# Norming, transposing and evacuating the tokens in two halves at the beginning of a hybrid decoder layer

## The chip, the cores and the metric

The kernel runs on one core of a Trainium2 chip. The metric is the device time of one execution in microseconds (us); lower is better. All times below are of the kernel before the change.

## The reference

One decoder layer with two branches over 16 meta tokens and 512 real tokens of width 1024. What matters here is its beginning:

```
h = concatenate([meta, x])                 # 528 tokens x 1024
u = h * rsqrt(mean(h*h) + eps) * norm_pre  # RMSNorm, row by row
proj = u @ w_in                            # 1024 x 12336 columns
z_ssd, xbc, dt_raw, z_att, q, k, v, f_raw, g_raw = split(proj)
xbc = silu(causal_depthwise_conv(xbc))     # holds x, B and C of the state space branch
dt = softplus(dt_raw + dt_bias); logf = log_sigmoid(f_raw + fgate_bias)
```

Then come a chunked state space scan (32 heads, chunks of 128), an attention with forget gates (16 heads), gates, three more products and a last RMSNorm with the residual. Everything is float32.

## The kernel before, in words

**Products.** Every float32 product is made of three: operands are split into a rounded part (`hi`) and the rest (`lo`), and `gemm` (L96) adds hi·hi, hi·lo and lo·hi. The tokens lie transposed, as `uhi` and `ulo`, 8 tiles (`k`) of 128 features by 528 tokens. `wpart` (L81) loads a block of 128 weight columns into a `raw` tile (three buffers), has ScalarE round it to `whi` and VectorE (GpSimd for the first one) make `wlo`; `whi` and `wlo` have two buffers each. A block for all tokens is 24 weight tiles times two spans of 264 tokens, that is 48 matmuls of 264 columns (L105).

**Beginning.** SyncE issues, in this order (L148 to L153): the meta tokens, token tile 0, `norm_pre`, token tiles 1 and 2, `conv_w`, `conv_b`, token tile 3, `ssd_norm`, `gate_bias`. Then come the 48 columns of `w_in` for dt and f (L167, L168: rows of 128 and 64 bytes), and then the blocks of `wpart`. An issue can wait for the landing of the one eight places ahead of it. Each token tile (128 tokens by 1024) is squared and summed on ScalarE (`square`, L208), gets its factor from a chain of small instructions (`rstd`, L177 to L181) and is multiplied on VectorE (`scaled`, L219). TensorE warms up with 8 products of zero consequence (L202), transposes the meta tokens (L232) and then, in 32 transposes (L250), the four tiles. The results of one `k` for all four tiles fill one bank of PSUM with 512 tokens. Eight pairs of instructions evacuate them: ScalarE writes `uhi` (L252), VectorE `ulo` (L253).

**First products.** The product for dt and f (`hdf`, `ldf`: 24 weight tiles of 48 columns, two spans) goes to two banks of the pool `ax` (4 banks, one each), which the transposes use too. It feeds a long chain of VectorE and ScalarE instructions (L295 to L369). The block C_B follows as the first of `ssd_gemm(0)`, in a buffer of the pool `mm` (2 buffers of two banks), with its convolution (`conv`, L375), then C_C and the others.

**Order.** The program is written as a flow of tiles; a planner lays out each engine's queue by its own forecast of times, higher priority first among what it holds ready. `raised(n)` sets the priority: token loads have 4, the norms, transposes and evacuations 3, the weight parts 1, the rest none. Once laid out, each queue is worked strictly in its order, whatever arrives first on the chip.

Of the kernel before, what the change touches and what calls it, by code (L numbers as in the profile page):

```python
# [8 lines left out]
F32 = mybir.dt.float32  # L9
# [4 lines left out]
ALU = mybir.AluOpType  # L14
# [3 lines left out]
P = 128  # L18
# [18 lines left out]
def hybrid_kernel(ctx, tc, x, meta, norm_pre, w_in, conv_w, conv_b, dt_bias, a_log, d_skip,  # L37
# [19 lines left out]
    def st(tag, shape, bufs, dt=F32):  # L57
        return sb.tile(shape, dt, tag=tag, name=nm(tag), bufs=bufs)
# [7 lines left out]
    def mm_ps():  # L66
        return mmp.tile([P, 2, 512], F32, tag="mm", name=nm("mm"))
# [10 lines left out]

    nparts = [0]

    def wpart(ap, kt=KD, slots=None):  # L81
        nparts[0] += 1
        n = ap.shape[1]
        raw = st("raw", [P, KD * P], BUFS["raw"])
        hi, lo = slots or [st(t, [P, KD * P], BUFS[t], F32R) for t in ("whi", "wlo")]
        raw, hi, lo = [t[:, 0:kt * n].rearrange("p (k n) -> p k n", k=kt) for t in (raw, hi, lo)]
        with raised():
            nc.sync.dma_start(out=raw, in_=ap.rearrange("(k p) n -> p k n", p=P))
            S.copy(hi, raw)  # L89
            (GP if nparts[0] <= 1 else V).tensor_sub(lo, raw, hi.bitcast(F32))  # L90
        return hi, lo
# [50 lines left out]
    def rows(o, ap):  # L142
        return o, ap.rearrange("o (t p) -> (o t) p", p=P)

    small = [[rows(prow2, norm_pre)], [],
             [(prow[0:96], conv_w.rearrange("o k (t p) -> (o k t) p", p=P)), rows(prow[96:120], conv_b)],
             [rows(prow3[0:16], ssd_norm), rows(prow3[16:32], gate_bias)]]
    with raised(4):  # L148
        nc.sync.dma_start(out=xt, in_=meta)
        for i in range(4):  # L150
            nc.sync.dma_start(out=htiles[i], in_=x[i * P:(i + 1) * P, :])
            for o, a in small[i]:
                nc.sync.dma_start(out=o, in_=a)  # L153
# [6 lines left out]
    drow = row()[:, 0:32]  # L160
    nc.gpsimd.dma_start(out=drow, in_=d_skip[0].partition_broadcast(P))

    rdf = st("raw", [P, KD * P], BUFS["raw"])[:, 0:KD * 48].rearrange("p (k n) -> p k n", k=KD)
    hdf = st("whi", [P, KD * P], BUFS["whi"], F32R)[:, 0:KD * 48].rearrange("p (k n) -> p k n", k=KD)
    ldf = st("wlo", [P, KD * P], BUFS["wlo"], F32R)[:, 0:KD * 48].rearrange("p (k n) -> p k n", k=KD)
    with raised():
        nc.sync.dma_start(out=rdf[:, :, 0:32], in_=w_in[:, C_DT:C_DT + 32].rearrange("(k p) n -> p k n", p=P))  # L167
        nc.sync.dma_start(out=rdf[:, :, 32:48], in_=w_in[:, C_F:C_F + 16].rearrange("(k p) n -> p k n", p=P))  # L168
        S.copy(hdf, rdf)
        GP.tensor_sub(ldf, rdf, hdf.bitcast(F32))  # L170

# [65 lines left out]
    V.tensor_mul(umv, tm[:, 0:P].rearrange("p (k n) -> p k n", n=NM), nb)  # L237
    S.copy(uhi[:, :, 0:NM], umv)
    V.tensor_sub(ulo[:, :, 0:NM], umv, uhi[:, :, 0:NM].bitcast(F32))
    for i in range(4):  # L240
        h = htiles[i]
        if i:
            square(S, h, sst[:, i:i + 1], 0)
        scaled(h, sst[:, i:i + 1], parts=2 if i == 3 else 1)

    ma, mb = mm_ps(), mm_ps()
    tps = [ax_ps(), ax_ps(), ma[:, 0], mb[:, 0], ax_ps(), ax_ps(), ma[:, 1], mb[:, 1]]
    for i in range(4):
        for k in range(KD):
            PE.transpose(tps[k][:, i * P:(i + 1) * P], htiles[i][:, k * P:(k + 1) * P], ident)  # L250
    for k in range(KD):
        S.activation(uhi[:, k, NM:L], tps[k], AF.Copy, scale=npre[:, k:k + 1])  # L252
        V.scalar_tensor_tensor(ulo[:, k, NM:L], tps[k], npre[:, k:k + 1],  # L253
                               uhi[:, k, NM:L].bitcast(F32), op0=ALU.mult, op1=ALU.subtract)
# [142 lines left out]

    def ssd_gemm(g):
        bt, ct = row("xbc"), row("xbc")
        conv(all_tokens(wcols(C_B + g * P)), 16 + g, bt)  # L400
        conv(all_tokens(wcols(C_C + g * P)), 20 + g, ct)
        xs, zs = [], []
        for j in range(4):
            t = row("xbc")
            conv(all_tokens(wcols(C_XS + g * 512 + j * P)), 4 * g + j, t)
            xs.append(t)
        for j in range(4):
            t = row("z", (P, T))
# [411 lines left out]
```

## Time and profile before

| | us |
|---|---|
| median of 3 runs (869.09 to 870.65) | 870.57 |
| profiled execution, its own time | 868.41 |
| span of the profile | 866.7 |
| TensorE busy in the span | 846.2 (98%) |
| VectorE busy | 596.3 (69%) |
| ScalarE busy | 434.3 (50%) |
| granted TensorE clock, mean | 0.999 |

The span runs from the first to the last instruction; 1.71 us of the execution's time lie outside it. PE is TensorE's matmul, PEld its weight load, DVE is VectorE, ACT is ScalarE, POOL is GpSimd, SP is SyncE. Matmuls overlap: their pace, not their duration, counts.

### The profile page before, as it was taken

Reading aid. Unit: us, or ns where it says so; the run is one execution under the profiler, and the core shown is the slowest. Engines: PE = TensorE matmul, PEld = TensorE weight load, DVE = VectorE, ACT = ScalarE, POOL = GpSimd, SP = SyncE. Lnnn points to the kernel's source line nnn. Section 1 sums busy time; section 2 is a strip of 40 time slices with the busy share of each in tenths; the row PEclk is TensorE's granted clock in tenths of the full one; section 3 lists DMA queues with packets and bytes.
Section 4 is the critical chain, followed back from the end, with each engine's and each line's share of the span. In section 5 each row is a group of like instructions: output and inputs, shape, how many; then the busy total and the mean of one; then the engine's idle time right before and its main releaser. Section 6 shows DMA issues by size and latency. Waiting matters only on the chain.

```text
span 866.7 us, 13656 instructions
## 1 busy us (share of the span) xinstructions
PE 846.2 (98%) x5277; PEld 737.6 (85%) x5277; DVE 596.3 (69%) x1228; ACT 434.3 (50%) x850; POOL 69.1 (8%) x136
## 2 busy tenths in 40 slices
PE   5999999999999999999999999999999999999997
PEld 4998888778987799777889898989899888888896
DVE  7799598847985689655765566666657564568735
ACT  6455365445632465334435565656566554543332
POOL 3030110010001100011001000000001000000000
PEclk9999999999999999999999999999999999999999
DMA  7254353335322543212223323232323222224422
GB/s 211 74 144 140 96 104 97 96 84 112 98 89 82 109 101 98 83 50 76 73 74 76 97 65 83 67 81 69 80 71 79 75 74 74 73 74 148 144 74 97
DMA packets 116548, 79.96 MB, mean 92 GB/s; under 512 B 5684, under 2 KB 112356, under 8 KB 116484
## 3 DMA queue, kind: packets, MB, share of 16 engines
q1 hardware_dynamic: 112740, 70.08, 28.6%
q0 software_dynamic: 3744, 9.01, 5.0%
q8 instruction: 41, 0.67, 0.3%
q14 instruction: 23, 0.19, 0.1%
HBM read 76.65 MB, written 2.44 MB: 91 GB/s over the span
## 4 chain that ended last, share of the span: by engine, by line
PE 90%; DVE 3%; DMA 3%; issue 3%; SPq 0%; POOL 0%; ACT 0%; DVEq 0%; POOLq 0%
PE mm L105 69%; PE ax L647 3%; PE mm L751 3%; PE ax L751 3%; PE ax L624 2%; DMA big<-acs_d 2%; PE ax L481 1%; PE ax L466 1%; PE ax L602 1%; PE ax L601 1%; PE ax L456 1%; PE ax L440 1%; PE ax L621 1%; DMA big<-in_x_dram 1%; DVE big L451 1%
## 5 line engine op out<-in xcount | busy, mean ns | idle before, releaser
L105 PE MATMUL mm<-ulo,whi 128*128 128x264 f32 (+1 forms) x1024 | 287.8, 329 | 0.0
L105 PE MATMUL mm<-uhi,whi 128*128 128x264 f32 (+1 forms) x1024 | 284.8, 328 | 0.4 <-DVE xbc L550 0.4
L89 ACT CAST whi<-raw 128x1024 fp32r<-128x1024 f32 x118 | 124.0, 1051 | 155.3 <-PE mm L105 104.8
L105 PE MATMUL mm<-uhi,wlo 128*128 128x264 f32 (+1 forms) x1024 | 191.6, 329 | 0.0
L105 PEld LDWEIGHTS mm<-uhi,whi 128*128 128x128 f32 x1024 | 172.6, 188 | 19.1 <-issue 2.9
L105 PEld LDWEIGHTS mm<-ulo,whi 128*128 128x128 f32 x1024 | 172.8, 188 | 17.7 <-issue 2.7
L90 DVE TENSOR_TENSOR wlo<-raw,whi 128x1024 fp32r<-128x1024 f32 x117 | 142.8, 1220 | 61.9 <-ACT whi L89 33.9
L105 PEld LDWEIGHTS mm<-uhi,wlo 128*128 128x128 f32 x1024 | 154.0, 188 | 17.0 <-issue 0.7
L105 PE MATMUL mm<-yhi,whi 128*128 128x512 f32 x192 | 78.6, 410 | 0.7 <-ACT ms L665 0.7
L105 PE MATMUL mm<-ylo,whi 128*128 128x512 f32 x192 | 76.7, 399 | 0.0
L607 ACT ACTIVATE tmp<-tmp,nmx 128x264 f32<-128x264 f32 (+3 forms) x80 | 41.3, 517 | 32.6 <-DVE nmx L604 27.5
L384 DVE SCALAR_TENSOR_TENSOR xbc<-xp,hcol,xbc 128x528 f32<-128x528 f32 x72 | 54.0, 761 | 0.7 <-ACT xbc L381 0.4
L105 PE MATMUL mm<-yhi,wlo 128*128 128x512 f32 x192 | 53.8, 400 | 0.0
L635 DVE TENSOR_TENSOR big<-ax,big 32x512 fp32r<-32x512 f32 (+1 forms) x64 | 37.3, 617 | 23.8 <-ACT big L634 23.1
L451 DVE TENSOR_SCALAR big<-big,dtok 128x128 f32<-128x128 f32 x128 | 28.6, 290 | 27.6 <-DMA big<-acs_d 27.6
L604 DVE CUSTOM_DVE_ANT_0 tmp<-ax,maskf 128x264 f32<-128x264 f32 (+3 forms) x80 | 32.5, 431 | 21.5 <-PE ax L602 21.1
L460 ACT ACTIVATE tmp<-ax,eac 128x64 f32<-128x64 f32 x128 | 28.2, 329 | 35.3 <-PE ax L456 35.3
L105 PEld LDWEIGHTS mm<-yhi,whi 128*128 128x128 f32 x192 | 36.1, 188 | 10.7 <-issue 2.3
L105 PEld LDWEIGHTS mm<-ylo,whi 128*128 128x128 f32 x192 | 36.1, 188 | 9.5 <-issue 2.6
L105 PEld LDWEIGHTS mm<-yhi,wlo 128*128 128x128 f32 x192 | 35.8, 188 | 9.4 <-issue 2.2
L634 ACT CAST big<-ax 32x512 fp32r<-32x512 f32 (+1 forms) x64 | 28.9, 522 | 27.1 <-PE ax L621 26.9
L667 DVE TENSOR_TENSOR ms<-ms,mm 128x512 f32<-128x512 f32 x24 | 16.5, 686 | 25.4 <-PE mm L105 25.4
(256 smaller groups left out, 1178.8 us busy)
## 6 DMA issues: line engine op xcount, KB each, us to landing
raw<-in_w_in_dram SPq DMA_DIRECT2D x88, 512.0 KB, 3.8
big<-acs_d POOLq DMA_DIRECT2D x16, 512.0 KB, 6.2
raw<-in_w_proj_ssd_dram SPq DMA_DIRECT2D x16, 512.0 KB, 3.4
raw<-in_w_proj_att_dram SPq DMA_DIRECT2D x8, 512.0 KB, 3.4
raw<-in_w_out_dram SPq DMA_DIRECT2D x8, 512.0 KB, 3.4
big<-in_x_dram SPq DMA_DIRECT2D x4, 512.0 KB, 6.1
yhi<-in_x_dram SPq DMA_DIRECT2D x2, 1024.0 KB, 7.6
out_dram<-big SPq DMA_DIRECT2D x3, 512.0 KB, 2.6
```

What stands on the lines that cost most here:

```text
L89: S.copy(hi, raw)
L90: (GP if nparts[0] <= 1 else V).tensor_sub(lo, raw, hi.bitcast(F32))
L105: PE.matmul(o, lw, u[:, a:b], start=i == 0, stop=i == len(seq) - 1)
L384: V.scalar_tensor_tensor(o, xp[:, k:k + L], cw[:, 24 * k + ct:24 * k + ct + 1], o, op0=ALU.mult, op1=ALU.add)
L451: V.tensor_scalar(ab[:, i], ab[:, i], ac_t[:, c, g * HG + i:g * HG + i + 1], 0.0, op0=ALU.subtract, op1=ALU.min)
L460: S.activation(y[:, i * 64:(i + 1) * 64], py[:, i * 64:(i + 1) * 64], AF.Copy, scale=eac[:, c, g * HG + i:g * HG + i + 1])
L604: V.tensor_tensor_reduce(pr[i][:, a:b], o, m, -1.0, 3e38, ALU.add, ALU.min, nmx[:, n:n + 1])
L607: S.activation(pr[i][:, a:b], pr[i][:, a:b], AF.Exp, bias=nmx[:, i:i + 1], scale=-1.0, accum_out=rsum[:, n:n + 1])
L634: S.copy(h, src)
L635: V.tensor_sub(l, src, h.bitcast(F32))
L647: PE.matmul(po[:, o:T], w, p, start=i == 0, stop=i == len(seq) - 1)
L751: PE.matmul(pss[s][t], a, b, start=kh == 0 and i == 0, stop=kh == 1 and i == len(seq) - 1)
```

## The change

The tokens are now normed, transposed and evacuated in two halves of 256 (token tiles 0 and 1, then 2 and 3). The product for dt and f and the block C_B are each made one span at a time, in turns. Both now go to `mm` buffers. The loads on SyncE have a new order: meta, tile 0, `norm_pre`, tile 1, the dt and f columns, tile 2, the block C_B, tile 3; the other parameters follow with a lower priority.

```
-    def wpart(ap, kt=KD, slots=None):
+    def wpart(ap, kt=KD, slots=None, loaded=None):
...
-        raw = st("raw", [P, KD * P], BUFS["raw"])
+        raw = loaded if loaded is not None else st("raw", [P, KD * P], BUFS["raw"])
...
     with raised(4):
         nc.sync.dma_start(out=xt, in_=meta)
...
+        x_load(0)
+        nc.sync.dma_start(out=small[0][0], in_=small[0][1])
+        x_load(1)
+        nc.sync.dma_start(out=rdf[:, :, 0:32], in_=w_in[:, C_DT:C_DT + 32].rearrange("(k p) n -> p k n", p=P))
+        nc.sync.dma_start(out=rdf[:, :, 32:48], in_=w_in[:, C_F:C_F + 16].rearrange("(k p) n -> p k n", p=P))
+        x_load(2)
+        nc.sync.dma_start(out=raw0.rearrange("p (k n) -> p k n", k=KD),
+                          in_=w_in[:, C_B:C_B + P].rearrange("(k p) n -> p k n", p=P))
+        x_load(3)
+    with raised(2):
+        for o, a in small[1:]:
+            nc.sync.dma_start(out=o, in_=a)
...
-    for i in range(4):
-        h = htiles[i]
-        if i:
-            square(S, h, sst[:, i:i + 1], 0)
-        scaled(h, sst[:, i:i + 1], parts=2 if i == 3 else 1)
-
-    ma, mb = mm_ps(), mm_ps()
-    tps = [ax_ps(), ax_ps(), ma[:, 0], mb[:, 0], ax_ps(), ax_ps(), ma[:, 1], mb[:, 1]]
-    for i in range(4):
+    def half(j):
+        for i in (2 * j, 2 * j + 1):
+            if i:
+                square(S, htiles[i], sst[:, i:i + 1], 0)
+            scaled(htiles[i], sst[:, i:i + 1])
+        tps = [ax_ps().rearrange("p (k n) -> p k n", k=2) for _ in range(4)]
+        for i in range(2):
+            for k in range(KD):
+                PE.transpose(tps[k // 2][:, k % 2, i * P:(i + 1) * P],
+                             htiles[2 * j + i][:, k * P:(k + 1) * P], ident)
+        c = slice(NM + 256 * j, NM + 256 * (j + 1))
         for k in range(KD):
...
+            o = tps[k // 2][:, k % 2]
+            S.activation(uhi[:, k, c], o, AF.Copy, scale=npre[:, k:k + 1])
+            V.scalar_tensor_tensor(ulo[:, k, c], o, npre[:, k:k + 1], uhi[:, k, c].bitcast(F32),
+                                   op0=ALU.mult, op1=ALU.subtract)
+
+    half(0)
+    half(1)
...
-    dps = [ax_ps()[0:48, 0:HL] for _ in range(2)]
-    gemm(dps, (hdf, ldf), uh, ul, ALLT, True)
+    first = mm_ps()
+    dps = mm_ps()
+    dps, first = [dps[0:48, i, 0:HL] for i in range(2)], first[:, :, 0:HL]
+    w0 = wpart(w_in[:, C_B:C_B + P], loaded=raw0)
+    for i, span in enumerate(ALLT):
+        gemm([dps[i]], (hdf, ldf), uh, ul, [span], True)
+        gemm([first[:, i]], w0, uh, ul, [span])
...
-        conv(all_tokens(wcols(C_B + g * P)), 16 + g, bt)
+        conv(all_tokens(wcols(C_B + g * P)) if g else first, 16 + g, bt)
```

## Rows read from the trace of the kernel before

**Rows 1.** The page: the span in 40 equal slices, busy tenths of TensorE.

```profile
PE   5999999999999999999999999999999999999997
```

**Rows 2.** Busy time of each engine in five stretches of the span (us; x is the count of instructions; then the granted clock as a share of full speed, the DMA share and GB/s).

```profile
0.00:17.40 17.40, 8.74 (x51) 5.43 (x51) 11.85 (x46) 11.42 (x22) 7.59 (x19) 1.00 0.84 232
17.40:29.30 11.90, 11.76 (x96) 11.45 (x96) 5.88 (x11) 7.42 (x12) 0.19 (x1) 1.00 0.22 57
29.30:100.00 70.70, 70.70 (x480) 63.78 (x479) 64.38 (x114) 34.95 (x54) 11.84 (x24) 1.00 0.44 123
100.00:850.00 750.00, 744.69 (x4571) 646.89 (x4570) 505.24 (x1029) 377.00 (x749) 49.52 (x93) 1.00 0.32 86
850.00:866.70 16.70, 10.26 (x87) 10.06 (x85) 8.90 (x31) 3.50 (x15) 0.00 (x0) 0.96 0.32 126
```

**Rows 3.** The chain that ended last, in order of time, around the beginning (start, us, what).

```profile
3.97 6.99 DMA big<-in_x_dram
10.98 1.16 ACT yhi L208 x2
...
15.29 0.70 ACT uhi L252
...
16.01 2.07 DVE ulo L253 x3
...
24.72 27.23 PE mm L105 x224
```

**Rows 4.** TensorE in order of time: the warm-up, the first transposes of tile 0, those of tile 1 (first and last group), the first matmul of the dt and f product, and the first two of block C_C.

```profile
5.91 3.20 PE L202 MATMUL ax<-tmp,identb 128*128 128x512 bf16 x8 [5.91 <-DVE tmp L199]
...
9.81 0.33 PE L250 MATMUL ax<-ident,big 128*128 128x128 f32 x1
9.98 0.60 PE L250 MATMUL mm<-ident,big 128*128 128x128 f32 x4
...
11.42 0.44 PE L250 MATMUL ax<-ident,big 128*128 128x128 f32 x2 [0.73 <-DVE big L219]
...
12.13 0.38 PE L250 MATMUL ax<-ident,big 128*128 128x128 f32 x2
...
17.47 0.32 PE L105 MATMUL ax<-uhi,whi 128*48 128x264 f32 x1 [0.16 <-DVE ulo L253]
...
29.42 0.40 PE L105 MATMUL mm<-uhi,whi 128*128 128x264 f32 x2
```

**Rows 5.** ScalarE in order of time (start, us, what, in brackets its idle time before): the squares of token tiles 1, 2 and 3, the rounding of the dt and f columns and of block C_B, and the first evacuations.

```profile
7.67 1.06 ACT L208 ACTIVATE yhi<-big 128x1024 f32<-128x1024 f32 x1 [1.04 <-DMA big<-in_x_dram]
...
9.28 1.06 ACT L208 ACTIVATE yhi<-big 128x1024 f32<-128x1024 f32 x1
...
10.98 1.06 ACT L208 ACTIVATE yhi<-big 128x1024 f32<-128x1024 f32 x1 [0.22 <-DMA big<-in_x_dram]
...
12.37 0.50 ACT L169 CAST whi<-raw 128x384 fp32r<-128x384 f32 x1
...
14.10 1.05 ACT L89 CAST whi<-raw 128x1024 fp32r<-128x1024 f32 x1 [0.51 <-DMA raw<-in_w_in_dram]
15.29 2.42 ACT L252 ACTIVATE uhi<-ax,npre 128x512 fp32r<-128x512 f32 x4
```

**Rows 6.** VectorE in order of time: the first step for tile 1 with the multiplication of tile 0 behind it, the multiplications of tile 1 and of tile 3 (in two parts).

```profile
8.86 0.15 DVE L178 TENSOR_SCALAR msq<-sst 128x1 f32<-128x1 f32 x1 [1.58 <-ACT yhi L208]
8.95 0.81 DVE L219 TENSOR_SCALAR big<-big,rst,msq 128x1024 f32<-128x1024 f32 x1
...
10.55 0.81 DVE L219 TENSOR_SCALAR big<-big,rst,msq 128x1024 f32<-128x1024 f32 x1
...
14.33 0.99 DVE L219 TENSOR_SCALAR big<-big,rst,msq 128x512 f32<-128x512 f32 x2
```

**Rows 7.** Durations by line (ns min/median/max, first and last start in us): the evacuations of 512 columns, the nearest smaller reads of PSUM on ScalarE (64 columns) and VectorE (144 to 400 columns).

```profile
L252 ACT ACTIVATE uhi<-ax,npre x4: 679/687/696, 15.3 to 17.0; 128x512 fp32r<-128x512 f32 x4
...
L253 DVE SCALAR_TENSOR_TENSOR ulo<-ax,npre,uhi x4: 743/743/751, 16.0 to 18.2; 128x512 fp32r<-128x512 f32 x4
L253 DVE SCALAR_TENSOR_TENSOR ulo<-mm,npre,uhi x4: 740/742/751, 18.9 to 21.0; 128x512 fp32r<-128x512 f32 x4
...
L460 ACT ACTIVATE tmp<-ax,eac x128: 295/330/365, 96.3 to 398.3; 128x64 f32<-128x64 f32 x128
...
L604 DVE CUSTOM_DVE_ANT_0 tmp<-ax,maskf x80: 290/432/572, 427.0 to 771.0; 128x264 f32<-128x264 f32 x32, 128x144 f32<-128x144 f32 x16, 128x400 f32<-128x400 f32 x16, 128x272 f32<-128x272 f32 x16
```

**Rows 8.** Busy time of each engine and the DMA (last two columns: share, GB/s) in two short stretches: token tiles, and the dt and f columns.

```profile
7.50:9.50 2.00, 2.00 (x13) 0.93 (x11) 0.65 (x2) 1.66 (x4) 0.00 (x0) 1.00 1.01 320
9.50:11.50 2.00, 1.21 (x12) 0.89 (x11) 1.77 (x11) 1.75 (x4) 0.00 (x0) 1.00 1.02 130
```

**Rows 9.** Groups of instructions of the first 30 us, shapes kept apart (count | busy us, mean ns | idle before): the root and the reciprocal of a token tile's factor.

```profile
L177 ACT ACTIVATE sd<-sst,epsc 128x1 f32<-128x1 f32 x4 | 1.2, 294 | 0.1
...
L179 DVE RECIPROCAL rst<-sd 128x1 f32<-128x1 f32 x4 | 0.6, 157 | 0.2 <-ACT sd L177 0.2
```

**Rows 10.** ScalarE's first copy out of block C_B's buffer, by line as in rows 7.

```profile
L380 ACT COPY xp<-mm x1: 588/588/588, 30.1 to 30.1; 128x528 f32<-128x528 f32 x1
```

**Rows 11.** The longest that TensorE waited for after 20 us (us in total, times, longest), and the busy time of the engines between 40 and 60 us (columns as in rows 2).

```profile
PE ax L500 <- DVE tmp L497: 2.1, 1, 2.1
...
40.00:60.00 20.00, 20.00 (x167) 19.59 (x166) 19.79 (x33) 8.60 (x13) 5.13 (x11) 1.00 0.38 105
```

More of the change, by code (lines that the diff above doesn't have):

```diff
@@ L87, in wpart @@
         with raised():
-            nc.sync.dma_start(out=raw, in_=ap.rearrange("(k p) n -> p k n", p=P))
+            if loaded is None:
+                nc.sync.dma_start(out=raw, in_=ap.rearrange("(k p) n -> p k n", p=P))
             S.copy(hi, raw)
@@ L143, in rows, with x_load @@
         return o, ap.rearrange("o (t p) -> (o t) p", p=P)
-    small = [[rows(prow2, norm_pre)], [],
-             [(prow[0:96], conv_w.rearrange("o k (t p) -> (o k t) p", p=P)), rows(prow[96:120], conv_b)],
-             [rows(prow3[0:16], ssd_norm), rows(prow3[16:32], gate_bias)]]
+    small = [rows(prow2, norm_pre), (prow[0:96], conv_w.rearrange("o k (t p) -> (o k t) p", p=P)),
+             rows(prow[96:120], conv_b), rows(prow3[0:16], ssd_norm), rows(prow3[16:32], gate_bias)]
+    raw0 = st("raw", [P, KD * P], BUFS["raw"])
+    rdf = st("raw", [P, KD * P], BUFS["raw"])[:, 0:KD * 48].rearrange("p (k n) -> p k n", k=KD)
+    def x_load(i):
+        nc.sync.dma_start(out=htiles[i], in_=x[i * P:(i + 1) * P, :])
     with raised(4):
         nc.sync.dma_start(out=xt, in_=meta)
-        for i in range(4):
-            nc.sync.dma_start(out=htiles[i], in_=x[i * P:(i + 1) * P, :])
-            for o, a in small[i]:
-                nc.sync.dma_start(out=o, in_=a)
+        x_load(0)
[10 more added lines that the diff above has]
+            nc.sync.dma_start(out=o, in_=a)
     dfb = cst.tile([48, 1], F32, name="dfb")
@@ L161, in hybrid_kernel @@
     nc.gpsimd.dma_start(out=drow, in_=d_skip[0].partition_broadcast(P))
-    rdf = st("raw", [P, KD * P], BUFS["raw"])[:, 0:KD * 48].rearrange("p (k n) -> p k n", k=KD)
     hdf = st("whi", [P, KD * P], BUFS["whi"], F32R)[:, 0:KD * 48].rearrange("p (k n) -> p k n", k=KD)
@@ L166, in hybrid_kernel @@
     with raised():
-        nc.sync.dma_start(out=rdf[:, :, 0:32], in_=w_in[:, C_DT:C_DT + 32].rearrange("(k p) n -> p k n", p=P))
-        nc.sync.dma_start(out=rdf[:, :, 32:48], in_=w_in[:, C_F:C_F + 16].rearrange("(k p) n -> p k n", p=P))
         S.copy(hdf, rdf)
@@ L239, in hybrid_kernel @@
     V.tensor_sub(ulo[:, :, 0:NM], umv, uhi[:, :, 0:NM].bitcast(F32))
-    for i in range(4):
-        h = htiles[i]
-        if i:
-            square(S, h, sst[:, i:i + 1], 0)
-        scaled(h, sst[:, i:i + 1], parts=2 if i == 3 else 1)
-    ma, mb = mm_ps(), mm_ps()
-    tps = [ax_ps(), ax_ps(), ma[:, 0], mb[:, 0], ax_ps(), ax_ps(), ma[:, 1], mb[:, 1]]
-    for i in range(4):
-        for k in range(KD):
[L250 to L254, printed above, removed]
+    def half(j):
[9 more added lines that the diff above has]
+        c = slice(NM + 256 * j, NM + 256 * (j + 1))
+        for k in range(KD):
+            o = tps[k // 2][:, k % 2]
[4 more added lines that the diff above has]
+    half(1)
     pre.close()
```

## The prediction, made before the changed kernel ran

> **What bounds the kernel now.** I read the page's slices first: TensorE has a 9 in every slice but the first and the last [rows 1]. So TensorE's own stream is the bound, and only its idle stretches can be won. The table of stretches says where they are: 8.66 of the first 17.40 us, 5.31 of 750 in the middle, 6.44 in the last 16.7 [rows 2]. This change touches the first one. There I read the chain that ended last: the load of token tile 3 to 10.98, its square, its factor and multiplication, its transposes, the first evacuations at 15.29 and 16.01, and then nothing but matmuls [rows 3]. The first product starts at 17.47, block C_C at 29.42 [rows 4]; between them lie 96 matmuls in 11.90 us with 0.14 us idle, 0.1225 us each [rows 2]. I forecast the second of these two marks, C_C's start: a shift of it is a shift of the end as long as TensorE stays full behind it. That it does is the reading of the next stretch, busy 70.70 of 70.70 us [rows 2].
>
> **The change part by part.** *First half, when it is ready.* Tiles 0 and 1 come ahead of every moved load, so they land as before: tile 1's square starts on its landing at 7.67 [rows 5]. Its multiplication ended at 11.36 [rows 6], its transposes ran from 11.42 to 12.51 [rows 4]. Two `k` now share a bank, and the first bank is full after the first two transposes of tile 1, at 11.86. One evacuation of 256 columns isn't in the trace. On ScalarE it lies between half of the 512-column one, 0.34, and that one, 0.69; a straight line from 64 columns (0.33) to 512 gives 0.48 [rows 7], which I take. On VectorE it lies between 0.37 and 0.74; the forms of L604, from 0.29 for 144 columns to 0.57 for 400, give 0.41 at 256 [rows 7]; with its third operand I take 0.45. So the first matmul can go at 11.86 + 0.48 + some 0.1 = 12.4, against 17.47. It needs `hdf`: its load now goes before tile 2 and its rounding takes 0.50 [rows 5], so it is there.
>
> *More evacuation work.* 16 x 0.45 instead of 8 x 0.743 on VectorE is +1.3 us (0 to +5.9), 16 x 0.48 instead of 8 x 0.69 on ScalarE is +2.2 us (0 to +5.5). Half of it lies beside matmuls of the first half; it is felt as pace: a `k` gives the dt and f product three matmuls, 0.37 us, and costs VectorE 0.45.
>
> *Second half, later than now.* Tile 3 gets two things ahead of it. The dt and f columns (48 x 1024 x 4 bytes = 197 KB) moved at 130 GB/s with the DMA engines fully busy: 1.5 us; at the 320 GB/s of token tiles it would be 0.6 [rows 8]. Block C_B (524 KB) takes 1.6 us at that rate; 1.9 is the upper end, from the rounding of the dt and f columns at 12.37, ahead of which these had landed, to 14.10, when C_B had, with a little before it [rows 5]. What leaves (76 KB of parameters) gives 0.2 back. Tile 3 then lands at 10.98 + 1.5 + 1.6 - 0.2 = 13.9; bounds 12.9 to 14.8. From landing to multiplied took 4.34 us (10.98 to 15.32) [rows 5, 6] with stalls in it; the instructions alone are about 2.9 (square 1.16 to its sum [rows 3], root 0.29 and four small ones by the 0.16 of the reciprocal [rows 9], multiplication 0.81 [rows 6]). So tile 3 is ready between 16.8 and 18.2, transposed by 17.7 to 19.1, evacuated 3.6 us later, 21.3 to 22.7. In the kernel before the last evacuation starts at 21.0 [rows 7]. The second half is thus no earlier than the whole was; all that is won is matmuls of the first half done meanwhile.
>
> *TensorE's sum.* From 12.4 on it has 96 x 0.1225 = 11.8 us of matmuls as before, and what no longer lies ahead of the first one: 16 transposes of tiles 2 and 3 at 0.11 = 1.8, and the parameter transposes, 0.4. Never starved, C_C starts at 26.4. It is starved a little: the first dt and f product goes at VectorE's 0.45 per `k`, 8 x 0.08 = 0.6; and block C_B must be rounded, 1.05 us on ScalarE [rows 5], behind eight evacuations (from 11.9 to 15.8) and perhaps tile 3's square: 16.8 to 18.1, where the first dt and f product and tile 2's transposes are through at about 16.9. I take 0.4 of the 0 to 1.2. C_C starts at 27.4: 2.0 us gained. Bounds of this case: 3.4 (starved only for part of the pace) to 1.0.
>
> *Edits costed at nothing.* That the products moved to `mm` buffers: C_C needs one of the two. The dt and f buffer is free first, read by ScalarE while 2.9 us of C_B's second span run. If C_C had to take C_B's buffer instead, it would wait for its copy, 0.59 us [rows 10] plus 0.3: 0.9 us. The weights of C_C need the `whi` of dt and f, which is free that same 2.9 us ahead and takes 1.05 to refill [rows 5]. The late parameters land about 15 us, ahead of the first convolution. The load order costs SyncE nothing, as only nine issues of some 0.45 us lie ahead of tile 3.
>
> *Total.* The profiled execution took 868.41 us, span 866.7 and 1.71 outside; it becomes 866.4. The runs' median is 2.16 above it, so against the median 870.57 the forecast is 868.5.
>
> **The rivals.** *(a) The half waits for the whole on ScalarE.* Queues are worked in the planner's order, and it has misjudged arrivals here: VectorE stood 1.58 us before the first step for tile 1, with tile 0's multiplication queued behind it [rows 6]. If tile 3's square is queued ahead of the first half's evacuations, these wait for tile 3's landing: 13.9 + 1.16 = 15.1, first matmul 15.6, and 11.8 + 1.8 + 0.4 behind it make 29.6. That is +0.2: 870.8. For it: that stall. Against it: evacuations are written ahead of that square, and three loads lie between tiles 1 and 3.
>
> *(b) Slower: TensorE's queue holds tile 3's transposes ahead of the first half's products.* They have the higher priority, and would be placed as soon as the planner believes tile 3 multiplied. Nothing then starts before 17.9 (tile 3 at 13.9 + 2.9, 8 transposes), and 11.8 + 0.4 more is 30.1, +0.7 us. And TensorE has stood most of the time from 12.5 on. Coming out of its first 5.91 us of idleness it ran 8 matmuls of 512 columns in 3.20 us, 0.40 each, the pace of 1.2 GHz, although the granted clock of that stretch is given as 1.00; the first transpose at 9.81 still took 0.33 us, those from 9.98 on 0.27 [rows 4]. Such a restart lasted 4.07 us, at half speed 2.0 us lost: 870.57 + 0.7 + 2.0 = 873.3. It decides from the point where the idleness brings the clock down; gaps of 0.73 [rows 4] did not.
> The Trainium skill, "TensorE: Matmul & The Clock Gate", Part 1, states that the throttled state is the default and that activity releases it, idleness brings it back; by it the 2.0 us are due in this case and only in this one. The trace agrees for the start; no row shows a fall later on.
>
> *(c) Won and lost again.* VectorE is busy 19.79 of 20 us between 40 and 60 [rows 11], with the chain behind dt and f, which starts only about 1 us earlier. Were a matmul to wait for it there, the gain ends between 0 and 1 us: 870.0. Against it: the longest of TensorE's later waits is 2.1 [rows 11], and VectorE has 6.3 us to spare up to 100 us [rows 2].
>
> *(d) More.* The planner's new order also takes away one of the later waits, 2.1 us [rows 11]: 866.4.
>
> **How the numbers follow.** Forecast 0.57, (a) 0.19, (b) 0.12, (c) 0.09, (d) 0.03. 0.2% is 1.74 us, about what a measurement can tell from no change. The forecast's gain of 1.0 to 3.4 lies mostly above it: 0.41 faster, 0.16 within; with (d) faster is 0.44. Within: 0.16, most of (a) 0.17 and (c) 0.08, and 0.01 of (b): 0.42. Slower: 0.11 of (b), 0.02 and 0.01 of the others: 0.14. The range starts at the forecast's best, 867.2, less 0.8 for the scatter of the runs (half of 1.56), 866.4, and ends within (b) at 872.2, which leaves out its dearer half.
>
> **What would show it.** First matmul of L105 near 12.4, not after 15; tile 3's square at 13.9; transposes of tiles 2 and 3 standing between products, after most of the first dt and f product; C_C's first matmul at 27.4; `uhi` evacuations of 0.48 and `ulo` of 0.45; and the next 70 us of TensorE full. The prediction is wrong if C_C starts at 29 or later, or if it starts earlier and the end does not follow.

## The result: slower, and the profile after

The changed kernel takes 875.15 us (median of 4 runs, 874.62 to 876.11) against 870.15 of the kernel before (4 runs beside it): a ratio of 1.0057, interval 1.0042 to 1.0071. Forecast was 868.5. The profiled executions are 874.62 against 868.41, spans 872.9 against 866.7. Executions of one kernel differ by up to 6.7 us, the longer ones at a lower mean granted clock (the kernel before: from 867.68 at 0.998 to 872.32 at 0.994), and one execution of the last kernel below, 1315.22 us at 0.609, is left out of its figures. The profiled execution of before is among its shortest, so the profiles lie 6.2 apart and the medians 5.0.

The five stretches, columns as in [rows 2]:

```profile
0.00:17.40 17.40, 7.83 (x41) 4.52 (x41) 13.23 (x46) 12.02 (x25) 7.58 (x19) 1.00 0.89 238
17.40:29.30 11.90, 11.32 (x81) 11.05 (x82) 6.33 (x15) 4.10 (x10) 0.00 (x0) 0.86 0.12 37
29.30:100.00 70.70, 67.37 (x450) 60.01 (x448) 61.91 (x111) 35.48 (x49) 11.19 (x22) 1.00 0.44 117
100.00:850.00 750.00, 745.63 (x4573) 647.20 (x4572) 505.51 (x1024) 379.36 (x754) 50.88 (x95) 1.00 0.32 87
850.00:872.90 22.90, 16.47 (x140) 16.27 (x138) 11.83 (x41) 5.93 (x21) 0.00 (x0) 0.97 0.23 92
```

The loss has two places. Up to 29.3 us TensorE did less, at a granted clock of 0.86 in the second stretch. From 29.3 to 100, full before, it stands 3.33 us (70.70 less 67.37). Behind 100 us nothing of weight changes.

**The first place.** TensorE in order of time, answering to [rows 4]: warm-up, transposes of the first half (one group of 16), first product, the transposes of the second half, the last matmul of the dt and f product, the first of C_C.

```profile
7.74 3.57 PE L213 MATMUL ax<-tmp,identb 128*128 128x512 bf16 x8 [7.74 <-DVE tmp L210]
12.03 1.97 PE L259 MATMUL ax<-ident,big 128*128 128x128 f32 x16
14.75 0.32 PE L106 MATMUL mm<-uhi,whi 128*48 128x264 f32 x1 [0.76 <-ACT uhi L264]
...
17.98 0.41 PE L259 MATMUL ax<-ident,big 128*128 128x128 f32 x2 [0.84 <-DVE ulo L265]
...
20.26 1.49 PE L259 MATMUL ax<-ident,big 128*128 128x128 f32 x6
...
22.89 0.60 PE L259 MATMUL ax<-ident,big 128*128 128x128 f32 x4
...
29.41 0.29 PE L106 MATMUL mm<-ulo,whi 128*48 128x264 f32 x1
...
32.48 0.40 PE L106 MATMUL mm<-uhi,whi 128*128 128x264 f32 x2
```

C_C starts at 32.48, 3.06 us after the 29.42 of before, although the first product starts 2.72 us earlier. The stretch from 14 to 22 us by the microsecond (columns as in [rows 2]) tells what lies between:

```profile
14.00:15.00 1.00, 0.25 (x2) 0.25 (x3) 1.00 (x1) 1.00 (x6) 1.00 (x1) 1.00 1.19 306
15.00:16.00 1.00, 0.32 (x3) 0.10 (x1) 0.96 (x6) 0.97 (x3) 0.03 (x1) 1.00 1.00 239
16.00:17.00 1.00, 0.86 (x5) 0.58 (x5) 1.00 (x7) 0.95 (x3) 0.00 (x0) 1.00 0.68 79
17.00:18.00 1.00, 0.16 (x3) 0.05 (x1) 1.00 (x4) 0.91 (x2) 0.00 (x0) 1.00 0.82 250
18.00:19.00 1.00, 1.00 (x7) 0.94 (x8) 1.00 (x3) 0.00 (x0) 0.00 (x0) 0.71 0.70 211
19.00:20.00 1.00, 1.00 (x6) 0.98 (x5) 0.73 (x2) 0.00 (x0) 0.00 (x0) 0.50 0.00 0
20.00:21.00 1.00, 1.00 (x7) 1.00 (x6) 0.00 (x0) 0.07 (x1) 0.00 (x0) 0.50 0.00 0
21.00:22.00 1.00, 1.00 (x7) 0.97 (x6) 0.48 (x1) 0.62 (x2) 0.00 (x0) 0.59 0.00 0
```

From 15 to 18 TensorE stands 0.68 + 0.14 + 0.84 = 1.66 us. The 0.84 at 17.98 comes from the order of TensorE's queue: two transposes of the second half stand there ahead of the first half's next products, and they wait for a bank of `ax` that a `ulo` evacuation still reads. Then the clock falls to 0.50, its lower level, just as work arrives: 0.29 + 0.50 + 0.50 + 0.41 = 1.70 us lost. With the prediction's own 14.0 us of matmuls and transposes behind the first product, 14.75 + 14.0 + 1.66 + 1.70 is 32.1; the chip shows 32.48.

Why starved? ScalarE and VectorE in order of time:

```profile
12.99 1.06 ACT L219 ACTIVATE yhi<-big 128x1024 f32<-128x1024 f32 x1 [0.40 <-DMA big<-in_x_dram]
...
14.23 0.47 ACT L264 ACTIVATE uhi<-ax,npre 128x256 fp32r<-128x256 f32 x1
...
20.93 0.48 ACT L264 ACTIVATE uhi<-ax,npre 128x256 fp32r<-128x256 f32 x1 [2.98 <-PE ax L259]
```

```profile
13.13 1.92 DVE L278 COPY dcol<-tmp 64x16 f32<-64x16 f32 x1
...
15.54 0.48 DVE L265 SCALAR_TENSOR_TENSOR ulo<-ax,npre,uhi 128x256 fp32r<-128x256 f32 x1
...
17.75 0.80 DVE L230 TENSOR_SCALAR big<-big,rst,msq 128x1024 f32<-128x1024 f32 x1
...
25.86 0.48 DVE L265 SCALAR_TENSOR_TENSOR ulo<-ax,npre,uhi 128x256 fp32r<-128x256 f32 x1 [0.15 <-ACT uhi L264]
```

The first evacuation stands on ScalarE behind tile 3's square (12.99). The first `ulo` comes 1.31 us after its `uhi`, behind a copy of 64 by 16 elements (`dcol`, the skip weights) that takes 1.92 us. Tile 3 is multiplied at 17.75, between `ulo` evacuations. Its transposes then stand in TensorE's queue between products: ScalarE waits 2.98 us for them at 20.93, and the last `ulo` starts at 25.86, where before it started at 21.0 [rows 7].

**The second place.** All that TensorE waited for between 29.3 and 100 us (us in total, times, longest):

```profile
PE mm L106 <- DVE z L432: 2.7, 2, 1.6
PE mm L106 <- ACT xp L400: 0.5, 1, 0.5
```

The waits on `z` are two. The third of the four `z` products needs the `mm` buffer of the first, which is free once VectorE has made `z` from it (L432). The block behind the `z` products waits in the same way for VectorE's third `z` step. The first `z` product and the two that waited, then VectorE's first `z` step, in the changed kernel:

```profile
63.91 0.40 PE L106 MATMUL mm<-uhi,whi 128*128 128x512 f32 x1
...
79.57 0.50 PE L106 MATMUL mm<-uhi,whi 128*128 128x512 f32 x1 [1.57 <-DVE z L432]
...
92.27 0.51 PE L106 MATMUL mm<-uhi,whi 128*128 128x264 f32 x2 [1.10 <-DVE z L432]
```

```profile
78.84 0.67 DVE L432 SCALAR_TENSOR_TENSOR z<-z,mm 128x512 f32<-128x512 f32 x1
```

The same two marks in the kernel before:

```profile
59.73 0.40 PE L105 MATMUL mm<-uhi,whi 128*128 128x512 f32 x1
```

```profile
71.49 0.67 DVE L412 SCALAR_TENSOR_TENSOR z<-z,mm 128x512 f32<-128x512 f32 x1
```

From product to step it is 14.93 us in the changed kernel and was 11.76 in the kernel before. VectorE's queue has fallen back 3.2 us against TensorE's. It falls back early: from 30 to 40 us it is busy 6.93 of 10 us, where it was 9.93 before, as the dt and f chain starts later. The long instruction of that chain, a reciprocal, before and after:

```profile
29.80 3.44 DVE L308 RECIPROCAL tmp<-tmp 48x528 f32<-48x528 f32 x1
```

```profile
36.34 3.44 DVE L328 RECIPROCAL tmp<-tmp 48x528 f32<-48x528 f32 x1
```

### The profile page after: what moved, and what is told of

Its sections match the earlier page's. It is cut to its first block, busy times and chain, and to the rows that moved or that the text cites. A ratio compares the mean times of both kernels' runs of the same rounds, so it can differ in the third digit from the quotient of the medians.

```text
span 872.9 us, 13676 instructions
## 1 busy us (share of the span) xinstructions
PE 848.6 (97%) x5277; PEld 739.1 (85%) x5277; DVE 598.8 (69%) x1235; ACT 436.9 (50%) x858; POOL 69.6 (8%) x136
## 4 chain that ended last, share of the span: by engine, by line
PE 88%; DVE 5%; issue 3%; DMA 2%; ACT 1%; SPq 1%; POOL 0%; DVEq 0%; POOLq 0%; ACTq 0%
PE mm L106 68%; PE ax L667 3%; PE mm L771 3%; PE ax L771 3%; PE ax L644 2%; PE ax L501 1%; PE ax L476 1%; DMA big<-acs_d 1%; PE ax L486 1%; PE ax L622 1%; PE ax L621 1%; PE ax L460 1%; PE ax L641 1%; DMA big<-in_x_dram 1%; DVE big L471 1%
## 5 line engine op out<-in xcount | busy, mean ns | idle before, releaser
L106 PE MATMUL mm<-uhi,whi 128*128 128x264 f32 (+2 forms) x1040 | 290.9, 328 | 4.5 <-DVE z L432 2.7
L106 PE MATMUL mm<-ulo,whi 128*128 128x264 f32 (+2 forms) x1040 | 294.5, 330 | 0.8 <-DVE ulo L265 0.8
L106 PEld LDWEIGHTS mm<-uhi,whi 128*128 128x128 f32 (+1 forms) x1040 | 175.4, 188 | 24.7 <-DVE z L432 3.4
L106 PE MATMUL mm<-uhi,wlo 128*128 128x264 f32 (+2 forms) x1040 | 196.4, 328 | 0.0
L106 PEld LDWEIGHTS mm<-ulo,whi 128*128 128x128 f32 (+1 forms) x1040 | 175.7, 188 | 18.1 <-issue 2.3
L106 PEld LDWEIGHTS mm<-uhi,wlo 128*128 128x128 f32 (+1 forms) x1040 | 155.9, 187 | 17.1 <-issue 0.9
```

The source lines that it names most:

```text
L106: PE.matmul(o, lw, u[:, a:b], start=i == 0, stop=i == len(seq) - 1)
```

## The experiments

Ratios are to the kernel before, run beside them; "z mark" is the start of VectorE's first `z` step less that of the first `z` product (before 11.76, changed 14.93).

**Is it the late dt and f product?** Theory A: its end (29.41 against some 24.5) delays the chain behind it. The changed kernel with both dt and f spans written first:

```
     for i, span in enumerate(ALLT):
         gemm([dps[i]], (hdf, ldf), uh, ul, [span], True)
+    for i, span in enumerate(ALLT):
         gemm([first[:, i]], w0, uh, ul, [span])
```

> The changed kernel with one edit: both spans of the dt and f product are written ahead of both spans of block C_B. Theory A: half of the loss comes late, because the turns put the second span of dt and f at the very end of the beginning (it ends at 29.5 us instead of 24.5), the chain behind it starts VectorE's long work 6.5 us later (first step after the exponential at 35.8 instead of 29.3), VectorE becomes the bound up to 90 us and TensorE waits 3.2 us for it between 44 and 93 us. By A that step moves to about 33, the waits of TensorE between 29 and 100 us fall below 1 us, C_C still starts near 32.5, and the time falls by 2 to 3 us to about 872.5. Theory B (everything comes from the start, the loads and halves): C_C and the waits stay, time 875 as the changed kernel.

Measured 876.24, 1.0069 (1.0054 to 1.0084). The product still ended at 29.65, C_C started at 32.94, and the waits stayed at 3.2: the second half came so late that the planner filled in C_B's matmuls all the same. The edit did not move what it was to move. The opposite edit did, the kernel before with C_B's product written ahead of dt and f:

```
+    first = all_tokens(wcols(C_B))
     dps = [ax_ps()[0:48, 0:HL] for _ in range(2)]
     gemm(dps, (hdf, ldf), uh, ul, ALLT, True)
```

> The kernel before with one edit: block C_B's product is written ahead of the dt and f product, so that the latter ends with it, as in the changed kernel; no halves, old loads. Theory A (the late chain behind dt and f, not the beginning, costs 3.2 us): the beginning keeps its length, C_C starts at 29.4 to 30; the reciprocal of the chain moves from 29.8 to about 35.5, VectorE is busy nearly throughout from there to 90 us, TensorE's waits between 33 and 100 us go from 0 to about 3 us, and the time is about 3 us above the kernel before, 872.7. Theory B (the beginning alone): no waits between 33 and 100, time within 0.7 us of the kernel before.

Measured 868.87, 0.9999 (0.9987 to 1.001). VectorE in order of time: C_B's taps, then the dt and f chain:

```profile
30.60 1.57 DVE L385 SCALAR_TENSOR_TENSOR xbc<-xp,hcol,xbc 128x528 f32<-128x528 f32 x2 [0.21 <-ACT xbc L382]
...
33.22 0.76 DVE L385 SCALAR_TENSOR_TENSOR xbc<-xp,hcol,xbc 128x528 f32<-128x528 f32 x1
...
35.62 3.45 DVE L309 RECIPROCAL tmp<-tmp 48x528 f32<-48x528 f32 x1
```

The reciprocal is nearly as late as in the changed kernel (35.62 against 36.34; before 29.80), yet TensorE doesn't wait: theory A falls. But C_B's three taps stand ahead of it here, while in the changed kernel VectorE has neither until 36.34, and the taps come behind (39.71, 42.05, 43.35). That was the hint for a later run.

**Is it the loads?** Theory B. The changed kernel with the old order of loads, and the kernel before with the new one:

```
-        x_load(1); dt and f columns; x_load(2); block C_B; x_load(3)
+        x_load(1); x_load(2); conv_w, conv_b; x_load(3); ssd_norm, gate_bias; dt and f columns; block C_B
```

> The changed kernel with the order of the loads put back: all four token tiles and the parameters first, then the dt and f columns, then block C_B. Theory B: tile 3's late landing (12.99 us instead of 10.98) holds up ScalarE's queue, with the first evacuations behind its square, and the second half. By B the first evacuation goes from 14.2 to about 12.5, C_C starts about 2 us earlier, near 30.5, and the time falls by about 2 us to 873. Rival: the second half is late because its transposes stand in TensorE's queue behind products and behind the evacuations of the first half; then C_C stays within 0.7 us of 32.5 and the time within 1 us of 875.

> The kernel before with the new order of loads alone; no halves, no turns. Theory B: tile 3 lands at about 13.0 instead of 10.98, everything behind it shifts by 2.0 us: C_C starts at 31.4 instead of 29.4, the time is 2 us above the kernel before, 872.2. Rival (the loads are hidden, the loss is all from halves and turns): within 0.5 us of the kernel before.

Old loads in the changed kernel: 874.08, 1.0049 (1.0034 to 1.0064). In its profiled execution C_C starts at 30.57, 1.9 us earlier, but the first product doesn't (14.77), and the waits stay at 3.3. Its clock falls earlier, to 0.58, 0.50, 0.50 and 0.72 in the four us from 12, after TensorE had stood 1.81 us ahead of 12.12; behind the first product it is at 1.00, and TensorE's gaps there are 0.71 us in sum. So the fall lies mostly ahead of the first product here, and 0.95 us of the 1.66 went behind it. In time the gain doesn't show (1.0049 against 1.0057, with intervals that overlap). New loads alone in the kernel before: 871.6, 1.0022 (1.0012 to 1.0031). In the profiled execution, the slowest of the ten, TensorE stands 2.38 us for tile 3 and the granted clock is 0.50 behind it:

```profile
17.12 0.44 PE L261 MATMUL ax<-ident,big 128*128 128x128 f32 x2 [2.38 <-DVE big L230]
...
19.67 0.45 PE L106 MATMUL ax<-uhi,whi 128*48 128x264 f32 x1
```

The first product comes 2.2 us later than in the kernel before, and no wait appears up to 100 us. By the medians (1.0022) B holds for some 2 us of the first place; it has nothing to do with the second.

**Is it the late warm-up?** It starts at 7.74 instead of 5.91 [rows 4], as VectorE fills its operand (L210) later. Theory C: give that to GpSimd.

```
-    V.memset(wz, 1.0)
+    GP.memset(wz, 1.0)
```

> The changed kernel with the operand of the warm-up filled by GpSimd instead of VectorE, so that the eight warm-up products start near 2.5 us and not at 7.74. Theory C: the transposes of the first half (12.03 to 14.00) waited for the warm-up, as tile 1 was multiplied at 10.3. By C they run about 9.5 to 11.2, the first evacuation is then held by VectorE's queue alone (the transposed norm_pre at 12.7), the first product starts 0.5 to 1.5 us earlier than 14.75, and the time falls by up to 1 us to 874.2. Rival: first product held by tile 3's square in ScalarE's queue (until 14.1): no earlier than 14.5, time unchanged; and with a longer idle stretch after the warm-up the granted clock may fall earlier, which adds up to 1.5 us.

Measured 877.94, 1.0097 (1.0081 to 1.0114): the worst up to here. The warm-up started at 5.45, but TensorE then stood for 1.52 us at 13.24 and 1.56 us at 15.91, the granted clock was 0.50 from 13 to 19, and the first product came at 16.68. The edit moved more than the warm-up: with GpSimd's queue shifted, VectorE's first `dcol` copy took 2.25 us from 13.10, and ScalarE's evacuations began only at 16.10. An earlier warm-up alone thus brings no earlier product; what it would bring with the rest unmoved, no run shows.

**Is it the copy on VectorE?**

```
-    V.tensor_copy(dcol[0:64], drow[0:64, 0::2])
-    V.tensor_copy(dcol[64:128], drow[64:128, 1::2])
+    GP.tensor_copy(dcol[0:64], drow[0:64, 0::2])
+    GP.tensor_copy(dcol[64:128], drow[64:128, 1::2])
```

> The changed kernel with the two small copies of dcol moved from VectorE to GpSimd. In the changed kernel the first of them took 1.92 us (0.15 before) while GpSimd made block C_B's lo part (12.66 to 15.03). Theory D: this stall holds VectorE's queue, that is the first half's evacuation (first at 15.54) and tile 3's multiplication (17.75). By D the copies' place is free, the first ulo evacuation follows the first uhi one at about 14.7, tile 3 is multiplied about 1 us earlier, C_C starts 0.7 to 1.2 us earlier than 32.48, and the time falls by about 1 us to 874. Rival: the next VectorE instruction of that kind waits for GpSimd just as long, or the second half is held by TensorE's queue: no change within 0.5 us.

Measured 874.53, 1.0063 (1.0049 to 1.0078). The first product is no earlier (15.01), but `ulo` follows faster, TensorE is busy 0.79, 0.57 and 0.53 in the three us behind 15, the clock stays at 1.00, and C_C starts at 30.60, 1.9 us earlier. The waits stay at 3.2. What goes in this profile is 0.55 of the 1.66 us of starvation and about the clock's 1.70: a TensorE less starved did not lose its clock. In time no gain shows by itself (1.0063 against 1.0057).

**Is it the clock?** The changed kernel with 24 idle products, whose output is overwritten later, behind the first half's evacuations:

```
     half(0)
+    for k in range(KD):
+        for _ in range(3):
+            PE.matmul(dps[0:48, 1, 0:256], hdf[:, k], uhi[:, k, NM:NM + 256], start=True, stop=True)
     half(1)
```

> The changed kernel with 24 idle products (three per evacuated tile of the first half, 48 x 256, into a bank of dt and f that is written anew later) which fill TensorE's idle time between 14.0 and 18.0 us. Theory E: the granted clock fell to 0.50 from 18.3 to 21.6 us because TensorE was mostly idle in the 4 us before, and this made the products and transposes of that stretch take 1.6 us more. By E the granted clock stays at 1.00 from 12 to 30 us; what the products take in busy time (24 x 0.12 = 2.9 us) is partly covered by the idle time of 2.6 us, so that C_C starts between 31 and 33 and the time is between 873.5 and 875.5. Rival: the fall comes whatever TensorE does (the granted clock falls at the same place): C_C later than 34, time 877.

Measured 876.32, 1.009 (1.0073 to 1.0108). The same columns as above:

```profile
12.00:18.00 6.00, 5.88 (x34) 5.54 (x34) 5.78 (x17) 5.47 (x13) 2.37 (x1) 1.00 1.02 269
18.00:22.00 4.00, 4.00 (x37) 4.00 (x36) 2.33 (x6) 0.97 (x3) 0.00 (x0) 1.00 0.16 48
```

From 18 to 22 the clock holds where it fell without the idle products, which fits idleness as the cause of the fall, as the run with `dcol` on GpSimd does. The 1.00 of the first row tells less: the 16 transposes there took 3.67 us against 1.97 in the changed kernel, so TensorE went at the pace of the lower level up to about 16. C_C starts at 33.02, 0.54 later. The idle products took 24 x 0.12 = 2.9 us of TensorE and the slower transposes another 1.70, so the run does not tell what the idle products alone cost.

**Is it the new buffers?** The kernel before with the dt and f product in an `mm` buffer, its chain raised:

```
-    dps = [ax_ps()[0:48, 0:HL] for _ in range(2)]
+    dps = mm_ps()
+    dps = [dps[0:48, i, 0:HL] for i in range(2)]
```

> The kernel before with two edits: the dt and f product goes to an mm buffer, as in the change (its first matmul waited at 17.47 for a bank of ax), and the chain behind it up to the exponential gets priority 2. By the theory that the change's gain could be had in place: first product at about 16.2 instead of 17.5, dt and f through at 23.5 instead of 24.5, C_C 0.5 to 1.2 us earlier, no new waits: 0.5 to 1.2 us below the kernel before. Rival: the product is held by the evacuations' pace (last one ends at 21.8 as before): within 0.4 us.

Measured 875.34, 1.0065 (1.0052 to 1.0079): an experiment that made a wait of its own. In the kernel before the transposes hold both `mm` buffers until the last evacuation, so the product waited for it, and at half pace (0.44 for two matmuls) went on from there:

```profile
22.68 0.65 PE L105 MATMUL mm<-uhi,whi 128*48 128x264 f32 x2 [3.95 <-DVE ulo L253]
```

It says nothing on the changed kernel, whose transposes use `ax` alone, but shows again what a stretch of idleness costs: granted clock 0.54 over 19 to 26 us.

**The second place: order or amount?** By then every kernel with halves and turns had 3.2 to 3.6 us of waits before 100 us, and none without had any. The turns swapped, in the changed kernel:

```
-        gemm([dps[i]], (hdf, ldf), uh, ul, [span], True)
         gemm([first[:, i]], w0, uh, ul, [span])
+        gemm([dps[i]], (hdf, ldf), uh, ul, [span], True)
```

> The changed kernel with the two products of a turn swapped: C_B's half is written ahead of the dt/f product's. Theory F: the 3.3 us that TensorE waits between 33 and 100 us come from VectorE, which is full from 36 to 92 us and begins that stretch late, because the dt/f product and C_B end together behind the second half, their evacuations meet on ScalarE (4.98 us busy in 30 to 35), and C_B's three tap steps then stand behind the 3.4-us reciprocal. With C_B first its taps run by about 34.5, ahead of the reciprocal (after 37); VectorE's idle time in 30 to 40 falls from 3.1 us to under 1.5, the waits in 33 to 100 fall below 1 us, and the time from 875.2 to about 872.5 (871.5 to 873.5). Rival G: the waits belong to the late end of the tokens as such, whichever product is first: they stay at 3 us, and the time within 1 us of the changed kernel's.

Measured 871.61 (12 runs), 1.0027 (1.0012 to 1.0041). Two lines exchanged are worth 2.6 us by the ratios, each to its own runs of the kernel before (3.5 by the medians). All waits between 29.3 and 100 us, and VectorE's order:

```profile
PE ax L486 <- DVE tmp L466: 0.6, 1, 0.6
```

```profile
31.86 1.57 DVE L404 SCALAR_TENSOR_TENSOR xbc<-xp,hcol,xbc 128x528 f32<-128x528 f32 x2
...
37.70 3.45 DVE L328 RECIPROCAL tmp<-tmp 48x528 f32<-48x528 f32 x1
```

The taps run ahead of the reciprocal, VectorE has work from 31.86, the z mark is 13.41 and the third product finds its buffer free. Theory F holds on order and time, rival G falls. One number of F's missed: VectorE's idle time in 30 to 40 is 2.2 us, not under 1.5. It fell back by 1.65 us instead of 3.2, which was enough. The other side of F, less work for VectorE:

```
-            (GP if nparts[0] <= 1 else V).tensor_sub(lo, raw, hi.bitcast(F32))
+            (GP if nparts[0] <= 4 else V).tensor_sub(lo, raw, hi.bitcast(F32))
```

> The changed kernel with the low parts of the weights of C_C, XS0 and XS1 subtracted on GpSimd instead of VectorE: three instructions of 1.2 us leave VectorE in the stretch before 50 us. Theory F (VectorE's fullness makes the waits): with 3.6 us of work less, z's multiply-adds come some 3 us earlier and the 2.7 us of waits on them fall below 0.7; time about 872.5. Rival G (the waits come from the order of the chain, not from how much VectorE has to do): z0's multiply-add stays near 78.8 and the waits at 3 us; time about 875.

Measured 882.65, 1.0142 (1.0125 to 1.016). The z mark is 12.29 and the wait on `z` 0.3, as F said, though the first `z` step itself stood at 78.20, near where G had it; but TensorE waited 2.4 for `xp` copies instead, the first product came at 16.60, behind 16 transposes that took 3.68 us, and the planner's new order left 3.1 us of waiting on L559 much later. For the time it is inconclusive; for VectorE's share in the wait on `z` it agrees.

**All together.** Old loads, `dcol` copies on GpSimd, C_B first:

> Three mends at once on the changed kernel: the old order of loads, the two copies of the skip weights on GpSimd, and C_B's half ahead of the dt/f product's. The first two alone each brought the first product of C_C from 32.48 to 30.6. If they mend two different delays, C_C starts near 29.6 and TensorE waits less than 1 us up to 100: time 869.5 to 871.5, level with the kernel before. If both mend the same delay (the second half's transposes and evacuations), C_C stays near 30.5 and the time is about 871. If rival G holds, 3 us more: 873 to 874.

Measured 869.17 (12 runs) against 869.52 (23 runs): 1.0000 (0.9989 to 1.0011). The stretches:

```profile
17.40:29.30 11.90, 11.90 (x100) 11.70 (x99) 6.18 (x14) 6.15 (x12) 0.14 (x1) 1.00 0.17 45
29.30:100.00 70.70, 70.15 (x476) 61.89 (x475) 65.97 (x119) 37.36 (x60) 15.26 (x24) 1.00 0.47 126
```

Both places are mended: TensorE nearly full (70.15 of 70.70) at full clock, waits of 0.6, the last `ulo` at 23.3 instead of 25.86. C_C starts at 29.95; with C_B first alone it started at 32.34, so the first place's 2.4 us there is the difference of the two ratios too (1.0027 and 1.0000). The loss of 5 us is thereby accounted for. Which of the two mends of the first place is needed, or whether both are, no run shows: none has one of them together with C_B first. What remains is a draw: products start at 15.14 instead of 17.47, but 16 transposes that lay ahead of them now lie among them, and TensorE stands at times between.

**Is there a version that wins?** First dt and f ahead in the first turn and C_B in the second, so that the first product needn't wait for C_B's weights, whose cast it waited 0.61 us for at 15.14:

> The kernel of three mends with one more change: in the first turn the dt/f product's half stands ahead again, in the second turn C_B's. There the first product waited 0.61 us at 15.14 for the cast of C_B's weights, which come last in the old order of loads. With dt/f first it starts near 14.7, all else the same: C_C 0.4 us earlier, no waits from 33 to 100, about 868.8 (868.0 to 870.0) against 869.5 of the kernel before: faster by at most 0.1%. If the second half's chain sets the start instead, nothing is gained: 869.2. If the waits on z come back, because C_B's copy ends up behind the dt/f chain again, 871 to 872.

Measured 869.93, 1.0006 (0.9992 to 1.002). The first product starts at 14.06, but C_B's first matmul stands 0.93 us for that cast at 15.43, and in the profiled execution the clock fell at 16. Then 8 or 16 idle products in its gaps, written as the 24 above, and 8 in the kernel of three mends:

> The kernel with mended loads, copies and turns (dt/f first in the first turn, C_B first in the second) plus 8 idle products of 256 columns, one behind each evacuation of the first half, their output overwritten later. Theory H: what is left of the loss is the clock's fall near 17 us, which that kernel's executions show in part only: 867.3 to 870.3 with a mean clock of 0.994 and more, 871.6 to 873.8 with 0.992 and less. The products fill gaps of a TensorE that stands 0.35 to 0.55 of each us there, so they cost under 1 us (8 by 0.12). If H holds the granted clock stays 1.00 from 12 to 30 in the profile, the executions at 0.992 go away, and the median is near 868.7 (868.0 to 869.3), 0.1% under the kernel before. Rival I: 8 products are too few, the clock falls all the same: 870 to 871. Rival J: the products stand in the way of the real ones: no fall, yet 870.

> As the run with 8 idle products, with 16. If 8 are too few and 16 are enough (rival I), the clock stays at 1.00 here and falls there. The price is at most another 1.0 us (8 by 0.12): under H some 0.3 to 1.0 us more than with 8, 869.0 to 869.7; under J twice the price, 871.

> 8 idle products in the kernel with C_B first in both turns. Its first product waited for C_B's cast until 15.14; here the idle products take that place. Under H: no fall, median 868.3 to 869.0. Under J: 0.5 us or more above that kernel's undisturbed executions (868.1 to 869.2), so 869.5.

Measured 871.15, 1.0007 (0.9993 to 1.0021); 869.97, 1.0007 (0.9993 to 1.0021); 869.98, 1.0002 (0.9988 to 1.0015). All level; executions at a mean clock of 0.992 or less are still there in each, so theory H fails as it was put, and none beats the kernel before. The best execution of all was one of the 16-product kernel, 867.25. What gives an execution a good start remains open.

## Why the prediction was wrong

Two steps failed: C_C's start, forecast at 27.4, through its first term above all (the first half evacuated right behind its transposes), and the step from there to the end, that TensorE stays full in the next 70 us. The parts in order:

**First matmul at 12.4: came at 14.75.** Tiles 0 and 1 were not late; tile 1's square ran at 6.52, 1.15 us earlier than in [rows 5]. The step that failed is "11.86 + 0.48 + some 0.1", the evacuation right behind its transposes. On the chip tile 3's square stood ahead of all eight `uhi` evacuations in ScalarE's queue, which is rival (a)'s mechanism, and the first of them came at 14.23. With the landing as it was, 12.99, rival (a)'s sum gives 12.99 + 1.16 + 0.5 = 14.65. A second slip lies beneath it: "its transposes ran from 11.42 to 12.51" was carried over from the old trace, and they ran from 12.03 to 14.00, behind a warm-up 1.83 us later.

**Evacuations of 0.48 and 0.45: right.** By line (ns min/median/max):

```profile
L264 ACT ACTIVATE uhi<-ax,npre x16: 457/474/477, 14.2 to 25.3; 128x256 fp32r<-128x256 f32 x16
L265 DVE SCALAR_TENSOR_TENSOR ulo<-ax,npre,uhi x16: 465/476/485, 15.5 to 25.9; 128x256 fp32r<-128x256 f32 x16
```

**Tile 3's landing, 12.9 to 14.8: inside, at the early end** (its square at 12.99 and not at 13.9). The terms of that sum with the 1.9 in place of the 1.6 reach 14.2, not 14.8. "Tile 3 is ready between 16.8 and 18.2" was nearly right (multiplied 17.75 to 18.55), but by luck: from landing to multiplied took 5.56 us, not 2.9 to 4.34, and the early landing made up for it. **Second half evacuated by 21.3 to 22.7: wrong**, it took to 26.3. The prediction timed evacuation, "3.6 us later", as if transposes came at once; on the chip they stood in TensorE's queue between products, at half clock. With the causes mended the last `ulo` still ended at 23.8.

**"It is starved a little", 0.6 and 0.4: came to 1.66 us.** About 0.55 of it came through two small `dcol` copies that no step looked at (1.11 are left with them on GpSimd); in the kernel before these had taken 0.15 and 0.17 us, at 11.79. Another 0.84 is the wait of the second half's transposes in TensorE's queue.

**The clock.** The forecast's sum had no term for a fall; it measured 1.70 us. Rival (b) gave 2.0 us for one, but tied it to tile 3's transposes holding up all the products. On the chip they held up some, for 0.84 of the 1.66 us, and the clock fell on starvation of that size. That gaps of 0.73 had not brought it down was no ground against 1.66 us of gaps in three. The Trainium skill, "TensorE: Matmul & The Clock Gate", Part 1, has idleness bring the lower level back; here the trace agrees in part, with 0.50 at 19 us after TensorE had stood 1.66 us of three, not throughout, and 1.00 from 18 to 22 where 24 products had filled the gaps.

**C_C at 27.4: came at 32.48**, by the three steps above: 2.35 late at the first product, 0.66 more starvation, 1.70 of clock, the rest 0.4. The upper bound of the gain, 3.4, was more than its own case without any starvation gives, 29.4 less 26.4, 3.0.

**"That it does is the reading of the next stretch, busy 70.70 of 70.70 us": wrong**, by 3.33 us, the larger half. That row holds for the old order, where VectorE had the dt and f chain's reciprocal from 29.80 and C_B's taps from 34.25. In the changed kernel both products end together, so neither gives VectorE work in time. Rival (c) named the engine, but had its chain "only about 1 us earlier" where it came 6.5 us later (the reciprocal 29.80 and 36.34), and was set aside by "VectorE has 6.3 us to spare up to 100 us", a sum: 6.0 of it lay behind 85 us. From 30 to 85 VectorE had 0.3 us, so what it loses at 30 it lacks at `z`. With C_B written first the waits on `z` are gone, and 0.6 us of waits is left in all. "C_C needs one of the two", the buffers' step, was right for C_C; its rate for `z` was not looked at.

**The signs.** The faster side had 0.44 and the slower 0.14; the prediction's own sign of being wrong, C_C at 29 or later, came true. Three rivals were each partly true at once, and their prices added; the forecast treated them as exclusive.

## What to carry to other kernels

Splitting a stage to start earlier pays only if the second part's preparation doesn't queue behind the first part's work on the same engine; look for what each in-order queue now holds ahead of the half that came late. When two chains come to end together, the order of the two in a full engine's queue can be worth more than the split: here two exchanged lines were worth about 3 us. A slack that is read as a sum over a stretch must be looked at by parts, and a cleared wait upstream says nothing about an engine that is full downstream.

## What the hardware showed that was not expected

A VectorE copy of 64 by 16 elements took 1.92 us, as long as GpSimd had a `wlo` subtraction to finish:

```profile
12.66 2.37 POOL L91 TENSOR_TENSOR wlo<-raw,whi 128x1024 fp32r<-128x1024 f32 x1 [2.95 <-ACT whi L90]
```

Both end at 15.0. On GpSimd itself, behind that subtraction, the copy took 0.26 us at 15.12, and VectorE's next operation there (L250) then took 0.71 instead of 0.28, to just behind the end of GpSimd's subtraction (15.17). The Trainium skill, "SBUF — State Buffer", section "SBUF: two separate sides", says that VectorE, for some kinds of its operations, and GpSimd share a pair of ports that the one which starts first holds for its whole instruction while the other stands; these runs agree.

The pace after the warm-up differs between executions although the granted clock is given as 1.00. TensorE in order of time, the runs with 8 and with 16 idle products:

```profile
11.83 2.92 PE L261 MATMUL ax<-ident,big 128*128 128x128 f32 x12 [0.44 <-DVE big L232]
...
18.52 0.42 PE L106 MATMUL mm<-uhi,whi 128*128 128x264 f32 x1
18.74 0.42 PE L106 MATMUL mm<-ulo,whi 128*128 128x264 f32 x1
```

```profile
17.39 0.29 PE L106 MATMUL mm<-uhi,whi 128*128 128x264 f32 x1
17.52 0.29 PE L106 MATMUL mm<-ulo,whi 128*128 128x264 f32 x1
```

At 18.5 us the first goes on at 0.22 us per matmul, the pace of 1.2 GHz; the second had 0.13 at 17.4, that of 2.4 GHz; both in stretches given as 1.00. Ahead of the first change on record it is the pace of equal matmuls that tells the level.
